# A trunk kernel on one core: vector and scalar work in instructions twice as wide

## The chip, the cores and the metric

The kernel runs on one core of a Trainium2 chip. A core has a matrix engine (TensorE, PE in the profile; its weight loads are listed apart as PEld), a vector engine (DVE), a scalar engine (ACT), GpSimd (POOL) and a queue engine (SP) that issues transfers. Each engine works through its own instructions in a fixed order and waits for the others at semaphores. The metric is the device time of one execution in microseconds (us), the median of several runs; lower is better.

## The reference

A decoder trunk of two layers over 256 tokens of width 1024, in float32. Cut to what matters:

```python
for l in range(DEPTH):                                      # 2 layers
    h = swiglu(x, w1[l, 0], w3[l, 0], w2[l, 0])             # (silu(x @ w1) * (x @ w3)) @ w2
    x = layernorm(ALPHA * x + 0.5 * h)
    h = mixer(x, l)
    x = layernorm(ALPHA * x + h)
    h = swiglu(x, w1[l, 1], w3[l, 1], w2[l, 1])
    x = layernorm(ALPHA * x + 0.5 * h)

def mixer(x):
    u, v, q, k, val, gates = split(x @ w_in)                # widths 1024, ..., 2 x 1024
    h_a = spatial_gate(gelu(u), layernorm(gelu(v)))         # 128x128 causal mixing of positions
    h_b = rmsnorm(diff_attention(rope(q), rope(k), val))    # 8 heads, two softmaxes subtracted
    g = sigmoid(gates + gate_b)
    return (g[0] * (h_a @ w_branch[0]) + g[1] * (h_b @ w_branch[1])) @ w_out
```

The hidden width of the SwiGLU is 2816. All weights are read once; nearly all arithmetic is in the matrix products.

## The kernel before

**Split products.** Each float32 operand is the sum of two rounded parts, hi and lo, and a product is hi·hi + lo·hi + hi·lo. The function `stream` fetches one transfer of weights, 128 partitions by up to 2048 float32 (1 MB), into a tile `raw` (four of them). It then splits it in two halves of 1024 columns: ACT copies a half into a tile `whi` (L166), DVE writes the rest, raw − whi, into a tile `wlo` (L168). There are eight tiles for hi halves and eight for lo halves, so a half's buffer is that of the same half four transfers earlier. With `sub=512` (in `gemm_b2`) each half is split in two pieces of 512.

**Projections by groups (`gemm_a2`).** x is held as `x_cat`, each k-tile with its 256 hi and 256 lo columns side by side. A group takes one or two transfers ("sources"), that is two or four halves, and each half has its own PSUM bank of 512 columns. First comes the hi phase: for each half eight matmuls of 512 columns (L220). Then the lo phase: for each half eight matmuls of 256 columns (L227) into the first half of the bank. After a half's last lo matmul ACT copies the bank's upper 256 columns to a tile r (L228) and DVE adds the lower 256 to it (L230, L232 where there is a scale). Four banks have the tag "main", so the bank of a half is free for the same half of the next group of two sources as soon as its add has run.

An FFN has 22 k-tiles of hidden width (FT). The first four come from `gemm_b2`, or from `gemm_first` at the start of the kernel, the other 18 from nine groups of two sources. After each source: silu on ACT (L523), the product on DVE (L524), and the split of the result into `hhi` (ACT, L173) and `hlo` (DVE, L174). Then two calls of `gemm_b`, one per half of the 1024 output columns, multiply by w2.

**`gemm_b`.** Both halves of the tokens (t = 0 and 1, 128 each) have a bank. The products of most k-tiles go to both in turn; the last k-tiles (tail, 4 unless the call says otherwise) are held back, and are done for t = 0 first, then `done(0)`, then for t = 1. In the FFN `done` reads the bank on DVE (L415, the residual and the first step of the norm). For the V projection of the mixer it is a Gelu on ACT (L688). `rows_b` issues the three products of a k-tile (L208).

**`gemm_b2`** does the same with four banks, two for each half of the tokens, and with the norm of the stage before running in its shadow. While that runs, some of its weight halves go to lent tiles of 512 columns from another pool (`lhi`, `llo`), since the normal ones aren't free yet. The norm's transposes (L474) are emptied by ACT into `xf` (L480), and `xf` is split into x (L173, L174).

**Mixer.** Eight rope groups of one source, then gates, V, u (groups of one source), the two branches (four groups of two sources), and the output by `gemm_b2`. Attention and the spatial gate run as side tasks: generators that issue a few instructions each time the main work has counted some beats (`beat`, `beside`). They use another four PSUM banks with the tag "side".

**Order.** PE's order is that of the program text. The order of DVE, ACT and POOL comes from a scheduler that goes by priorities (`step` raises them for each transfer), and `behind(...)` puts an instruction after a given one. SP issues the transfers.

Of the kernel before, what the change touches and what calls it, by code (L numbers as in the profile page):

```python
# [41 lines left out]
RAW, HL = 4, 8  # L42
# [8 lines left out]
def trunk(ctx, tc, x, xT, w13a, w13b, w2, wb, wqk, wa, wbr, wo, gateb, sgug, sgub, sguwT, sgubias, lam, diffg,  # L51
# [10 lines left out]
    act = ctx.enter_context(tc.tile_pool(name="act", bufs=27))  # L62
# [11 lines left out]
    def bank():  # L74
        return psum.tile([P, 512], F32, tag="main", name=name("bank"))
# [71 lines left out]
    def stream(src, width=CH, sub=HC, lent=(), after=(None, None)):  # L147
# [7 lines left out]
        for o in range(0, width, HC):  # L155
            if o // HC in lent:
                hi, lo = ([act.tile([P, 512], F32R, tag="slot", name=name(n)) for _ in range(2)] for n in ("lhi", "llo"))
                at = [(hi[j], lo[j]) for j in range(2)]
            else:
                hi = hi_pool.tile([P, HC], F32R, tag="hi", name=name("whi"))  # L160
                lo = lo_pool.tile([P, HC], F32R, tag="lo", name=name("wlo"))
                at = [(hi[:, p : p + sub], lo[:, p : p + sub]) for p in range(0, HC, sub)]
            for p, (h, w) in zip(range(0, HC, sub), at):
                r = raw[:, o + p : o + p + sub]
                with behind(latest[0]):
                    A.activation(h, r, AF.Copy)  # L166
                with behind(after[o // HC] or latest[1]):
                    V.tensor_tensor(out=w, in0=r, in1=h.bitcast(F32), op=ALU.subtract)  # L168
# [41 lines left out]
    def gemm_a2(srcs, xc, zs, rs=lambda: s512("r"), scale=1.0):  # L210
# [4 lines left out]
        for src in srcs:  # L215
            got += stream(src)
            for hi, _ in got[-2:]:
                b.append(bank())
                for k in range(KT):
                    PE.matmul(b[-1], hi[:, k * P : (k + 1) * P], xc(k), start=k == 0, stop=False)  # L220
                beat(0.65)
        for n, (_, lo) in enumerate(got):
            s = slice(n % 2 * T, (n % 2 + 1) * T)
            if n % 2 == 0:
                r, z = rs(), zs(n // 2)
            for k in range(KT):
                PE.matmul(b[n][:, :T], lo[:, k * P : (k + 1) * P], xc(k)[:, :T], start=False, stop=k == KT - 1)  # L227
            emptied[0] = A.activation(r[:, s], b[n][:, T:], AF.Copy, scale=scale).ins  # L228
            if scale == 1.0:
                a = V.tensor_tensor(out=z[:, s], in0=b[n][:, :T], in1=r[:, s], op=ALU.add)  # L230
            else:
                a = V.scalar_tensor_tensor(out=z[:, s], in0=b[n][:, :T], scalar=scale, in1=r[:, s], op0=ALU.mult,  # L232
                                           op1=ALU.add)
            added[0] = a.ins
            beat(0.35)
            if n % 2:
                yield n // 2, z
# [11 lines left out]
    def gemm_b(src, kts, xh, xl, done, tail=4, last=()):  # L249

        blocks = [[(bank(), c, n) for c, n in (last if t else ()) or ((0, 512),)] for t in range(NT)]
# [17 lines left out]
    def gemm_b2(srcs, xh, xl, done, norm=None):  # L269
# [3 lines left out]
        lent, after = [()] * 4, [(None, None)] * 4  # L273
        if norm:
            lent = [(0, 1), (0,), (), ()]
            after[1:3] = (None, norm.ends[0]), (norm.ends[0], norm.ends[0])
        ps = [[bank() for _ in range(2)] for _ in range(NT)]
# [16 lines left out]
    def gemm_first(srcs, done):  # L294

        step()
        ps = [[bank() for _ in range(2)] for _ in range(NT)]
        raw = [[raw_pool.tile([P, CH], F32, tag="raw", name=name("raw")) for _ in range(2)] for _ in range(2)]
        for k0, nk in ((0, 1), (1, 1), (2, 1), (3, 1), (4, 2), (6, 2)):
# [3 lines left out]
            if nk == 2 or k % 2 == 0:  # L303
                w = [[p.tile([P, HC], F32R, tag=n, name=name("w" + n)) for p, n in ((hi_pool, "hi"), (lo_pool, "lo"))]
                     for _ in range(2)]
# [187 lines left out]
    def ffn(l, f, i, norm, last=False):  # L493
# [26 lines left out]
        for j in range(FB, FT, 2):  # L520
            for m, z in gemm_a2([w13a[l, f, j - FB + m] for m in range(2)], both, lambda m: t512("silu")):
                s = z[:, :T]
                silu[0] = A.activation(s, s, AF.Silu).ins  # L523
                V.tensor_tensor(out=s, in0=s, in1=z[:, T:], op=ALU.mult)  # L524
                split(hh(j + m), hl(j + m), s)
                if norm is None and j + m == FB:
                    beside(setup(s[:, :1]), 0)
# [320 lines left out]
```

## Time and profile before

| | |
|---|---|
| median of 3 runs | 1243.45 us (1243.18 to 1244.18) |
| span of the profiled execution | 1242.5 us (its only time; 0.95 below the median) |
| PE busy | 1236.6 us, 6703 matmuls |
| DVE busy | 873.1 us, 1532 instructions |
| ACT busy | 756.0 us, 1388 instructions |
| POOL busy | 86.0 us |
| moved by DMA | 241.87 MB, 195 GB/s |

How to read it: busy time counts each engine by itself, and the engines run side by side. The span can't be shorter than the work of the engine that never rests. Matmuls overlap one another in a pipeline, so the step from one matmul's start to the next counts, not the duration of one record. In rows of the timeline the first number is the start, the second the time until the last of the xN instructions of that row ended, and in brackets stands the idle time of the engine before it and what ended it. In rows of groups the numbers after the first bar are the summed busy time and the mean nanoseconds of one.

### The profile page before, as it was taken

To read this page: it belongs to the slowest core of one execution; us is meant where nothing else is said; L and a number is where in the kernel's file an instruction comes from. 1 tells how busy PE (TensorE), PEld (TensorE's weight loads), DVE (VectorE), ACT (ScalarE), POOL (GpSimd) and SP (SyncE) were. 2 spreads that over 40 slices of the span, in tenths; PEclk is the share of its full clock that TensorE was granted. 3 is DMA by queue.
4 is the path that set the end of the run, shared out by engine and by line. 5 is a ranking of instruction groups with operands and counts; after the bars stand their busy time and mean duration, and the time that the engine had idled before them with its cause. 6 is when DMAs were issued, how large, how long until landed. Compare 5 with 4: busy or idle time off the path is not lost.

```text
span 1242.5 us, 17870 instructions
## 1 busy us (share of the span) xinstructions
PE 1236.6 (100%) x6703; PEld 1064.1 (86%) x6703; DVE 873.1 (70%) x1532; ACT 756.0 (61%) x1388; POOL 86.0 (7%) x184
## 2 busy tenths in 40 slices
PE   9999999999999999999999999999999999999998
PEld 8888888888888888888888888888888888888887
DVE  6766567876587977665677665679756879766753
ACT  6776446679665566664466664466786555766640
POOL 0100000144100000000000000002430000000000
PEclk9999999999999999999999999999999999999999
DMA  9765645654754745556545546556556456455540
GB/s 352 276 204 183 224 171 187 227 167 165 248 183 145 244 162 205 177 180 253 194 169 191 192 159 250 203 184 206 162 175 228 165 174 233 170 203 203 165 174 35
DMA packets 40679, 241.87 MB, mean 195 GB/s; under 512 B 5344, under 2 KB 6416, under 8 KB 14480
## 3 DMA queue, kind: packets, MB, share of 16 engines
q1 hardware_dynamic: 36624, 227.82, 52.1%
q0 software_dynamic: 3536, 12.13, 3.0%
q8 instruction: 52, 0.85, 0.3%
q10 hardware_dynamic: 432, 0.79, 0.2%
q14 instruction: 35, 0.29, 0.1%
HBM read 235.47 MB, written 1.05 MB: 190 GB/s over the span
## 4 chain that ended last, share of the span: by engine, by line
PE 99%; DVE 0%; ACT 0%; issue 0%; DVEq 0%; ACTq 0%
PE bank L220 38%; PE bank L208 35%; PE bank L227 20%; PE bank L323 2%; PE sbank L588 1%; PE sbank L474 1%; PE sbank L637 1%; PE sbank L718 1%; PE sbank L335 0%; PE sbank L635 0%; PE sbank L659 0%; PE sbank L508 0%; PE sbank L622 0%; PE sbank L627 0%; PE sbank L446 0%; DVE xtok L454 0%
## 5 line engine op out<-in xcount | busy, mean ns | idle before, releaser
L168 DVE TENSOR_TENSOR wlo<-raw,whi 128x1024 fp32r<-128x1024 f32 (+1 forms) x442 | 490.0, 1127 | 223.4 <-PE bank L227 129.3
L166 ACT ACTIVATE whi<-raw 128x1024 fp32r<-128x1024 f32 (+1 forms) x442 | 425.8, 978 | 279.4 <-PE bank L208 135.3
L220 PE MATMUL bank<-x,whi 128*128 128x512 f32 x1792 | 426.5, 392 | 0.0
L220 PEld LDWEIGHTS bank<-x,whi 128*128 128x128 f32 x1792 | 330.7, 188 | 69.0 <-issue 2.6
L227 PE MATMUL bank<-x,wlo 128*128 128x256 f32 x1792 | 229.9, 284 | 0.0
L227 PEld LDWEIGHTS bank<-x,wlo 128*128 128x128 f32 x1792 | 224.2, 191 | 4.8
L208 PE MATMUL bank<-whi,hhi 128*128 128x512 f32 (+1 forms) x374 | 141.3, 378 | 0.0
L208 PE MATMUL bank<-wlo,hhi 128*128 128x512 f32 (+1 forms) x374 | 141.0, 377 | 0.0
L208 PE MATMUL bank<-whi,hlo 128*128 128x512 f32 (+1 forms) x374 | 140.9, 377 | 0.0
L228 ACT ACTIVATE r<-bank 128x256 f32<-128x256 f32 x256 | 96.5, 380 | 66.0 <-PE bank L227 65.7
L208 PE MATMUL bank<-whi,x 128*128 128x512 f32 x328 | 106.6, 394 | 0.0
L208 PEld LDWEIGHTS bank<-whi,hlo 128*128 128x128 f32 x374 | 70.4, 188 | 13.0
L208 PEld LDWEIGHTS bank<-wlo,hhi 128*128 128x128 f32 x374 | 70.4, 188 | 12.7
L208 PEld LDWEIGHTS bank<-whi,hhi 128*128 128x128 f32 x374 | 70.4, 188 | 12.7
L208 PEld LDWEIGHTS bank<-whi,x 128*128 128x128 f32 x328 | 61.6, 188 | 12.7
L208 PE MATMUL bank<-wlo,x 128*128 128x512 f32 x164 | 64.0, 390 | 0.0
L480 ACT ACTIVATE xf<-sbank,ln_b,ln_g 128x128 f32<-128x128 f32 x80 | 30.0, 456 | 40.2 <-PE sbank L474 40.2
L230 DVE TENSOR_TENSOR silu<-bank,r 128x256 f32<-128x256 f32 x144 | 54.2, 418 | 0.2
L383 POOL DMA_DIRECT2D bc<-in_lng x6 | 3.2, 530 | 727.7 <-DVE bc L382 727.7
L415 DVE SCALAR_TENSOR_TENSOR xtok<-xtok,bank 128x512 f32<-128x512 f32 (+1 forms) x25 | 16.6, 663 | 42.2 <-PE bank L208 42.2
L564 POOL TENSOR_TENSOR swap<-swap,sin_t 128x512 f32<-128x512 f32 x16 | 24.3, 1517 | 242.4 <-DMA swap<-z 226.7
L208 PE MATMUL bank<-lhi,x 128*128 128x512 f32 x120 | 39.9, 396 | 0.0
(183 smaller groups left out, 1254.1 us busy)
## 6 DMA issues: line engine op xcount, KB each, us to landing
raw<-in_w13a SPq DMA_DIRECT2D x72, 1024.0 KB, 5.0
raw<-in_w SPq DMA_DIRECT2D x40, 1024.0 KB, 4.9
raw<-in_wa SPq DMA_DIRECT2D x24, 1024.0 KB, 5.5
raw<-in_wb SPq DMA_DIRECT2D x16, 1024.0 KB, 4.9
raw<-in_wqk SPq DMA_DIRECT2D x16, 1024.0 KB, 5.1
raw<-in_wbr SPq DMA_DIRECT2D x16, 1024.0 KB, 4.9
raw<-in_w13b SPq DMA_DIRECT2D x12, 1024.0 KB, 5.0
raw<-in_wo SPq DMA_DIRECT2D x8, 1024.0 KB, 4.9
```

Of the source, the lines that this page charges most:

```text
L166: A.activation(h, r, AF.Copy)
L168: V.tensor_tensor(out=w, in0=r, in1=h.bitcast(F32), op=ALU.subtract)
L208: PE.matmul(ps, xx, w, start=start and n == 0, stop=stop and n == 2)
L220: PE.matmul(b[-1], hi[:, k * P : (k + 1) * P], xc(k), start=k == 0, stop=False)
L227: PE.matmul(b[n][:, :T], lo[:, k * P : (k + 1) * P], xc(k)[:, :T], start=False, stop=k == KT - 1)
L228: emptied[0] = A.activation(r[:, s], b[n][:, T:], AF.Copy, scale=scale).ins
L230: a = V.tensor_tensor(out=z[:, s], in0=b[n][:, :T], in1=r[:, s], op=ALU.add)
L323: PE.matmul(ps[t][m], x[:, j, o + t * P : o + (t + 1) * P], y, start=k0 + j == 0 and o == 0 and y is hi, stop=k0 + j == KT - 1 and y is lo)
L415: V.scalar_tensor_tensor(out=self.y[t][:, s], in0=self.y[t][:, s], scalar=self.scale, in1=ps, op0=ALU.mult, op1=ALU.add)
L474: PE.transpose(b[:, k * P : (k + 1) * P], self.y[t][:, h * 512 + k * P : h * 512 + (k + 1) * P], ident)
L480: A.activation(xf[:, s], b[:, s], AF.Identity, scale=self.gT[:, f], bias=self.bT[:, f])
L564: turned_by[0] = G.tensor_tensor(out=s3, in0=s3, in1=s, op=ALU.mult).ins
```

## The change

- The tiles of `hi` and `lo` have 2048 columns, and there are four of each instead of eight. By default `stream` splits a whole transfer at once: one ACT copy and one DVE subtraction of 2048 columns. With `sub=512` pieces of 512 stay. The lent tiles are now given for whole transfers: the first two instead of one and a half. The pool they come from has 31 tiles instead of 27.
- `bank()` becomes `banks()`: one tile of two banks, two such tiles. In `gemm_a2` a source's two halves are the two banks of a tile, and r and the sum are made once for both (128x512 in two runs of 256).
- In the FFN, silu, product and split are done once for both sources of a group.
- In `gemm_b` the banks of t = 0 and t = 1 are the two banks of one tile (where the last call has two column blocks, a second tile is used).
- The matmuls, transfers and the order of PE's work are otherwise as before. `dynamic_dma_scratch_size=4096` is given to the program.

```diff
-RAW, HL = 4, 8
+RAW, HL = 4, 4
...
-    act = ctx.enter_context(tc.tile_pool(name="act", bufs=27))
+    act = ctx.enter_context(tc.tile_pool(name="act", bufs=31))
...
-    def bank():
-        return psum.tile([P, 512], F32, tag="main", name=name("bank"))
+    def banks():
+        return psum.tile([P, 2, 512], F32, tag="main", name=name("bank"), bufs=2)
...
-    def stream(src, width=CH, sub=HC, lent=(), after=(None, None)):
+    def stream(src, width=CH, sub=CH, lent=False, after=(None, None)):
...
-                hi = hi_pool.tile([P, HC], F32R, tag="hi", name=name("whi"))
-                lo = lo_pool.tile([P, HC], F32R, tag="lo", name=name("wlo"))
-                at = [(hi[:, p : p + sub], lo[:, p : p + sub]) for p in range(0, HC, sub)]
+                if o == 0:
+                    full = [p.tile([P, CH], F32R, tag=n, name=name("w" + n)) for p, n in ((hi_pool, "hi"), (lo_pool, "lo"))]
+                hi, lo = (v[:, o : o + HC] for v in full)
+                if sub == CH:
+                    at = [[v[:, :width] for v in full]][o:]
+                else:
+                    at = [(hi[:, p : p + sub], lo[:, p : p + sub]) for p in range(0, HC, sub)]
...
         for src in srcs:
             got += stream(src)
-            for hi, _ in got[-2:]:
-                b.append(bank())
+            b.append(banks())
+            for j, (hi, _) in enumerate(got[-2:]):
                 for k in range(KT):
-                    PE.matmul(b[-1], hi[:, k * P : (k + 1) * P], xc(k), start=k == 0, stop=False)
+                    PE.matmul(b[-1][:, j], hi[:, k * P : (k + 1) * P], xc(k), start=k == 0, stop=False)
                 beat(0.65)
-        for n, (_, lo) in enumerate(got):
...
+        for n, ps in enumerate(b):
+            r, z = rs(), zs(n)
+            for j, (_, lo) in enumerate(got[2 * n : 2 * n + 2]):
+                for k in range(KT):
+                    PE.matmul(ps[:, j, :T], lo[:, k * P : (k + 1) * P], xc(k)[:, :T], start=False, stop=k == KT - 1)
+                if j == 0:
+                    beat(0.35)
+            r2, z2 = (v.rearrange("p (j t) -> p j t", j=2) for v in (r, z))
+            emptied[0] = A.activation(r2, ps[:, :, T:], AF.Copy, scale=scale).ins
             if scale == 1.0:
-                a = V.tensor_tensor(out=z[:, s], in0=b[n][:, :T], in1=r[:, s], op=ALU.add)
+                a = V.tensor_tensor(out=z2, in0=ps[:, :, :T], in1=r2, op=ALU.add)
...
-        blocks = [[(bank(), c, n) for c, n in (last if t else ()) or ((0, 512),)] for t in range(NT)]
+        b = banks()
+        blocks = [[(b[:, 0], 0, 512)]]
+        if last:
+            b2 = banks()
+            blocks.append([((b, b2)[c > 0][:, 1], c, n) for c, n in last])
+        else:
+            blocks.append([(b[:, 1], 0, 512)])
...
         if norm:
-            lent = [(0, 1), (0,), (), ()]
+            lent = [True, True, False, False]
...
+            z = tmp.tile([P, 2, 2, T], F32, tag="pair", name=name("z"), bufs=1)
+            for _ in gemm_a2([w13a[l, f, j - FB + m] for m in range(2)], both, lambda m: z[:, m].rearrange("p j t -> p (j t)")):
+                pass
+            s = z[:, :, 0]
+            silu[0] = A.activation(s, s, AF.Silu).ins
+            V.tensor_tensor(out=s, in0=s, in1=z[:, :, 1], op=ALU.mult)
+            split(*(v[j // 2].rearrange("p (k t) -> p k t", k=2) for v in (h_hi, h_lo)), s)
```

What this does to DVE's order in a steady FFN group. Names carry a running number; `wlo` is the lo part of a transfer that is used two groups later, `bank` the PSUM tile, `r` ACT's copy of its upper columns, and in brackets stands whose semaphores the instruction waits for. DVE before:

```order
L168 TENSOR_TENSOR wlo_1175<-raw_1172,whi_1174 128x1024 [waits DMAHW0_49,PE_49]
L230 TENSOR_TENSOR silu_1013<-bank_966,r_1012 128x256 [waits Activation_49]
L230 TENSOR_TENSOR silu_1013<-bank_975,r_1012 128x256 [waits Activation_49]
L168 TENSOR_TENSOR wlo_1179<-raw_1172,whi_1178 128x1024
L524 TENSOR_TENSOR silu_1013<-silu_1013 128x256 [waits DVE_49,Activation_49]
L230 TENSOR_TENSOR silu_1039<-bank_994,r_1038 128x256 [waits Activation_49]
L230 TENSOR_TENSOR silu_1039<-bank_1003,r_1038 128x256 [waits Activation_49]
```

The same place on DVE after the change:

```order
L172 TENSOR_TENSOR wlo_1122<-raw_1119,whi_1121 128x2048 [waits DMAHW2_49,PE_49,Activation_49]
L236 TENSOR_TENSOR z_940<-bank_947,r_987 128x512 [waits DVE_49,Activation_49]
L236 TENSOR_TENSOR z_940<-bank_970,r_1006 128x512 [waits Activation_49]
L172 TENSOR_TENSOR wlo_1145<-raw_1142,whi_1144 128x2048 [waits DMAHW3_49]
L536 TENSOR_TENSOR z_940<-z_940 128x2x256 [waits Activation_49]
```

Before, a split of 1024 columns stands ahead of the first add, and it waits for PE; now a split of 2048 columns stands there, and the add behind it empties two banks.

PE at the end of the tail of an FFN's `gemm_b`, where the token half changes from t = 0 to t = 1. Before (bank 1592 is that of t = 0, 1593 that of t = 1):

```order
L208 MATMUL bank_1592<-whi_1694,hhi_155 128x512
L208 MATMUL bank_1592<-wlo_1695,hhi_155 128x512
L208 MATMUL bank_1592<-whi_1694,hlo_166 128x512
L208 MATMUL bank_1593<-whi_1664,hhi_149 128x512
L208 MATMUL bank_1593<-wlo_1665,hhi_149 128x512
L208 MATMUL bank_1593<-whi_1664,hlo_160 128x512
```

After (one tile, 1390, for both):

```order
L212 MATMUL bank_1390<-whi_1471,hhi_155 128x512
L212 MATMUL bank_1390<-wlo_1472,hhi_155 128x512
L212 MATMUL bank_1390<-whi_1471,hlo_166 128x512
L212 MATMUL bank_1390<-whi_1453,hhi_149 128x512 [waits DVE_49]
L212 MATMUL bank_1390<-wlo_1454,hhi_149 128x512
L212 MATMUL bank_1390<-whi_1453,hlo_160 128x512
```

The first matmul of t = 1 now waits for DVE; the instruction that it waits for is the read of the tile's other bank.

38 lines of the change are left out of this document (13 added, 25 removed).

## The prediction

> **What bounds the kernel now.** I read the busy line, the chain, the timeline of one FFN group, and then the groups that stand beside it. The first:
>
> ```profile
> span 1242.5 us, 17870 instructions
> PE 1236.6 (100%) x6703; PEld 1064.1 (86%) x6703; DVE 873.1 (70%) x1532; ACT 756.0 (61%) x1388; POOL 86.0 (7%) x184
> PE 99%; DVE 0%; ACT 0%; issue 0%; DVEq 0%; ACTq 0%
> ```
>
> PE is the bound: busy 1236.6 of 1242.5 us, and the chain is PE. All time in which PE does nothing is 5.9 us, so that is the most that smoother vector work can return as long as the matmuls keep their pace. DVE is at 70% and ACT at 61%; shortening them gives nothing by itself. The question is what the regrouped work does to PE's waits.
>
> One steady FFN group, PE alone and then all engines:
>
> ```profile
> 477.21 4.00 PE L227 MATMUL bank<-x,wlo 128*128 128x256 f32 x32
> 481.04 7.44 PE L220 MATMUL bank<-x,whi 128*128 128x512 f32 x32
> 488.32 4.00 PE L227 MATMUL bank<-x,wlo 128*128 128x256 f32 x32
> ...
> 488.52 1.06 ACT L166 ACTIVATE whi<-raw 128x1024 fp32r<-128x1024 f32 x1 [0.75 <-PE bank L220]
> 489.47 1.23 DVE L168 TENSOR_TENSOR wlo<-raw,whi 128x1024 fp32r<-128x1024 f32 x1 [3.81 <-PE bank L227]
> 490.62 0.75 DVE L230 TENSOR_TENSOR silu<-bank,r 128x256 f32<-128x256 f32 x2
> 491.28 1.22 DVE L168 TENSOR_TENSOR wlo<-raw,whi 128x1024 fp32r<-128x1024 f32 x1
> 492.15 1.32 PE L220 MATMUL bank<-x,whi 128*128 128x512 f32 x5
> ```
>
> A group is 32 wide matmuls with the hi weights, 7.28 us (481.04 to 488.32: 0.227 each), then 32 narrow ones with the lo weights, 3.83 us (488.32 to 492.15: 0.120 each), 11.11 together, and PE goes on without a gap. DVE, which had nothing to do, starts the next wlo 1.15 us into the lo phase: the eighth narrow matmul, which reads that buffer last, started at 488.32 + 7 × 0.120 = 489.16, so the release takes 0.31. Two adds take 0.75 us from 490.62 on; the first, which frees the first bank, ends at about 491.0, 1.1 us before PE needs the bank at 492.15. That 1.1 us is the slack of the present order.
>
> The durations:
>
> ```profile
> L168 DVE TENSOR_TENSOR wlo<-raw,whi 128x1024 fp32r<-128x1024 f32 x360 | 436.7, 1227 | 213.1 <-PE bank L227 126.8 <-ACT whi L166 70.7 <-issue 15.2
> L168 DVE TENSOR_TENSOR wlo<-raw,whi 128x512 fp32r<-128x512 f32 x82 | 53.3, 687 | 10.3 <-issue 7.9 <-PE bank L227 2.4
> L166 ACT ACTIVATE whi<-raw 128x1024 fp32r<-128x1024 f32 x360 | 378.2, 1059 | 225.8 <-PE bank L220 125.8 <-PE bank L208 91.5 <-ACT hhi L173 3.1
> L166 ACT ACTIVATE whi<-raw 128x512 fp32r<-128x512 f32 x82 | 47.5, 625 | 53.6 <-PE bank L208 43.8 <-PE bank L220 9.5
> L415 DVE SCALAR_TENSOR_TENSOR xtok<-xtok,bank 128x512 f32<-128x512 f32 x23 | 15.7, 684 | 39.1 <-PE bank L208 39.1
> L688 ACT ACTIVATE vg<-bank 128x512 f32<-128x512 f32 x8 | 4.8, 599 | 5.1 <-PE bank L208 5.1
> L688 ACT ACT_TABLE_LOAD x2 | 2.6, 1283 | 0.0
> ...
> 482.97 2.36 DVE L168 TENSOR_TENSOR wlo<-raw,whi 128x1024 fp32r<-128x1024 f32 x2
> ```
>
> **The wide split.** From 512 to 1024 columns the DVE subtract grows by 540 ns, so 2048 take about 1227 + 1080 = 2307 ns; four times 540 (2.16, no fixed part) and twice 1227 (2.45) bound it. Two in a row take 2.36, so the second starts 1.13 after the first, 0.09 before its end: the next instruction follows the wide one after about 2.22. In the same way ACT's 2048 is 1059 + 868 = 1.93 us (1.74 to 2.12). An add of 128x512 with a PSUM operand has its nearest row in L415: 0.68. By these rows the change saves on DVE 2 × 1.23 − 2.31 = 0.15 us a transfer, on ACT 0.19. That is worth nothing: PE covers it, and it waits for neither engine now.
>
> The Trainium skill ("Perfetto Trace Analysis", "Optimizing Scalar/DVE Operations") says that grouping into larger operations helps if the engine is saturated, and that where ScalarE and VectorE are not saturated but cause bubbles elsewhere, breaking instructions up lets work finish sooner. The DVE share of 70% puts this kernel in the second case, so by that rule too the sign is a loss.
>
> **FFN groups (the main term).** After the change DVE's order at the end of a group is: wlo of 2048 columns, add of the first tile, add of the second, wlo, multiply, hlo. Let L be the start of the lo phase.
> - The wlo writes the lo buffer that all 16 narrow matmuls of the first source read, not eight: it starts at L + 15 × 0.120 + 0.31 = L + 2.11 (now L + 1.15). The queue's order is fixed, so nothing passes it.
> - The add of the first tile stands behind it: L + 2.11 + 2.22 = L + 4.33, end at L + 5.01. ACT's copy r for it is ready: the whi ahead of it starts at L + 0.20 as at 488.52, ends at L + 2.13, and r (0.60) at L + 2.73.
> - The next group's first matmul writes that two-bank tile. There are two such tiles, so it waits for the add. PE resumes 0.13 after a DVE end (the boundary rows below: DVE ends 188.56 + 0.69 = 189.25, matmul at 189.38): L + 5.14, where it needs L + 3.84.
>
> So PE stalls 1.30 us a group. The second tile's add ends 0.6 later, while PE fills the first tile for 3.6 us: hidden. The period becomes 12.4 us, in which DVE has about 2 × 2.22 + 4 × 0.6 = 6.8 us: it catches up each time, and the stall neither grows nor heals. With 2.16 or 2.45 for the wide subtract it is 1.15 or 1.45. An FFN has 9 groups, four FFNs 36. In four of them, the first of each FFN, a piece hlo of 128x256 also stands ahead of the add:
>
> ```profile
> 38.12 0.42 DVE L174 TENSOR_TENSOR hlo<-sbank,hhi 128x256 fp32r<-128x256 f32 x1
> 38.46 0.75 DVE L230 TENSOR_TENSOR silu<-bank,r 128x256 f32<-128x256 f32 x2
> ...
> 178.91 0.39 PE L208 MATMUL bank<-whi,hhi 128*128 128x512 f32 x1
> 179.11 0.69 DVE L415 SCALAR_TENSOR_TENSOR xtok<-xtok,bank 128x512 f32<-128x512 f32 x1 [8.98 <-PE bank L208]
> ...
> 186.35 1.50 ACT L480 ACTIVATE xf<-sbank,ln_b,ln_g 128x128 f32<-128x128 f32 x4 [0.65 <-PE sbank L474]
> 188.56 0.69 DVE L174 TENSOR_TENSOR x<-xf,x 128x512 fp32r<-128x512 f32 x1 [1.08 <-ACT x L173]
> 188.93 0.39 PE L208 MATMUL bank<-lhi,x 128*128 128x512 f32 x1
> 189.38 0.65 PE L208 MATMUL bank<-lhi,x 128*128 128x512 f32 x2
> ```
>
> It takes 0.34 until the next starts (38.12 to 38.46), so these stall 1.64. Sum: 32 × 1.30 + 4 × 1.64 = 48.2 us (42 to 54 by the bounds). The mixer's four branch groups per layer have the same tiles; there one stands like an FFN group (1.30), one has 0.44 more work of PE behind it (0.86), and two have only two 512-wide pieces in front of the add, 2 × 0.60: 2.11 + 1.20 + 0.68 + 0.13 − 3.84 = 0.28 each. That is 2.7 a layer, 5.5 for two (0 if the neighbours cover it, 10.4 if all eight stall 1.30). The groups of one source wait for an add of the group before the last, with the whole next group (5.55 us) between: nothing.
>
> **The tails of the down projections.** The banks of the two token halves are now one tile, and the order shows the first matmul of the second half's tail waiting for DVE, which reads the first half's bank in that tile. Now PE runs straight on: at 178.91 it starts the second half, at 179.11 L415 reads the first. Then it must wait: 0.20 + 0.69 + 0.13 = 1.02 us, twice per FFN, eight times: 8.2 us. It is not hidden, since PE's queue has nothing else ahead. Bounds: 0, were the wait already met, and 8 × (1.02 + 2.22) if each L415 had a wide wlo in front of it. I take the place that the order gives, with none in front. The V projection waits in the same way for ACT's Gelu: 0.20 + 0.60 + 0.13 = 0.93 for the second half of columns; for the first the table load of 1.28 comes in between, up to 2.21, part of which (I take 0.5) passes while a whi copy and matmuls end: some 2.35 per layer, 4.7 in all (3.7 to 6.3).
>
> **The norm boundaries.** Where an FFN's norm feeds the next projection, x arrives just in time: DVE's x ends at 189.25, and the matmul at 189.38 follows. After the change four 512-wide whi pieces, which wait for a buffer of 2048 columns, stand in ACT's queue ahead of xf; I put x about 0.45 later, an estimate between nothing and one piece (0.63). Three places: 1.4 us (0 to 1.9).
>
> **The mixer's side work.** Attention steps (scores, softmax, transposes) pass through the same DVE and ACT queues. A step that finds itself behind a wide piece starts up to 2.31 − 1.23 = 1.08 us later. Eight head pairs in both layers with three hand-overs give at most 26 us, at least nothing, and a little below nothing if the saved 0.15 us arrives there. Tasks are spread over a group or more, so I lie near the low end: 2. DMAs are as many and as large as before, on the same queues; the smaller scratch for POOL's descriptors touches only loads that it issues long before use. Both: 0.
>
> **Sum.** 48.2 + 5.5 + 8.2 + 4.7 + 1.4 + 2 = 70.0 us on the profiled span of 1242.5, so 1312.5. The median of the runs, 1243.45, lies 0.95 above that span: 1313.4.
>
> **The rivals.**
>
> *Not slower: the matmuls get quicker.* The sum holds if a matmul costs what it costs now. Were the spacing limited by the vector engines' traffic, fewer and wider instructions could shorten it. 70 us over 6703 matmuls is 10.4 ns each; from there on the kernel is no slower (1243). Against it speaks a stretch in which both vector engines are idle:
>
> ```profile
> core 0: us, PE busy (x) PEld busy (x) DVE busy (x) ACT busy (x) POOL busy (x), PEclk, DMA share, GB/s
> 171.00:179.00 8.00, 8.00 (x37) 6.64 (x36) 0.00 (x0) 0.00 (x0) 0.00 (x0) 1.00 0.65 273
> ...
> 4.92 2.01 PE L323 MATMUL bank<-whi,x 128*128 128x512 f32 x4
> 6.77 0.63 PE L323 MATMUL bank<-wlo,x 128*128 128x512 f32 x2
> ```
>
> A record lasts 0.39, so a window of 8.00 us touches (8.00 + 0.39) / 0.227 = 37.0 of them: exactly the 37 counted. With DVE and ACT silent the spacing is the same 0.227 as in the group above, where both work. Chance 0.05. The Trainium skill ("TensorE: Matmul & The Clock Gate", "Wait — 56ns, not 53.3ns?") gives 215.7 ns for a warm matmul of 512 columns; by that figure 11 ns per wide matmul would be there to win, and the trace disagrees with it: 227 ns, vector engines idle or not.
>
> *Much slower: the clock falls at each wait.* At the start PE's four wide matmuls take 1.85 us (4.92 to 6.77), 0.46 each instead of 0.23, so a relapse of that length costs 0.9. On some 52 waits that is 47 us more, 1360. Against it: a wait of 1.3 in 12.4 us leaves PE busy for 90%; but the granted clock of 1.00 comes from stretches without such waits, so the trace doesn't exclude it. Chance 0.04.
>
> *The mixer pays more.* 10 to 26 us instead of 2, by the bound above: 1321 to 1337, in the middle 1329. For it: attention already waits on chains of small steps. Chance 0.15.
>
> *Only the groups pay.* The tails, branches and boundaries are covered after all, and the wide subtract is as short as 2.16: 1243.5 + 42 to 50, so 1286 to 1294. Against it: the waits stand in the order. Chance 0.10.
>
> **How the numbers follow.** My own sum holds with 0.66; its range, from the bounds of the subtract (±6), the V tail, the boundaries and the first few us of the mixer, is 1302 to 1324, and its middle is the prediction, 1313. To reach 0.8 I add the nearer parts of two rivals: down to 1292, up to 1336. Within 0.2%, 2.5 us, a measurement could not tell it from no change: 0.02. Faster 0.03, both from the first rival; slower 0.95.
>
> **What would show it.** In the profile after: PE's busy time nearly the same, its idle time 60 to 80 us; in the list of PE's waits DVE's add with some 40 times 1.3 us and L415's successor with eight times 1.0; wlo of 2048 columns at 2.3 us; a group period of 12.4 us; DVE's and ACT's busy time lower by some 40 and 60 us. Wrong would be: no wait of PE for the adds (DVE doing them ahead of the wlo), a wide matmul at less than 0.22 us, a granted clock under 1, or the largest wait in the mixer.

## The result, and the profile after

The changed kernel takes 1345.34 us (median of four runs, 1344.98 to 1346.59), the kernel before 1243.36: a ratio of 1.082, 95% interval 1.0805 to 1.0836. The direction was right; 1313 was 32 us too low, and the range ended at 1336.

The head of the profile's page and its chain, after:

```profile
span 1344.9 us, 16970 instructions
PE 1260.1 (94%) x6703; PEld 1068.0 (79%) x6703; DVE 851.3 (63%) x1156; ACT 702.4 (52%) x1012; POOL 86.8 (6%) x184
PE 75%; issue 8%; DVE 7%; ACT 5%; DMA 2%; POOL 2%; SPq 1%; DVEq 0%; ACTq 0%; POOLq 0%
```

DVE has become 21.8 us less busy and ACT 53.6, with a quarter fewer instructions. PE now rests 84.8 us instead of 5.9, and its own busy time has grown by 23.5 with the same 6703 matmuls. The list of PE's waits after (in total, how often, the longest):

```profile
PE bank L224 <- DVE z L236: 38.1, 32, 1.7
PE sbank L601 <- ACT aT L637: 14.2, 2, 7.1
PE bank L212 <- DVE xtok L425: 6.2, 8, 0.8
PE bank L212 <- DVE z L236: 4.5, 4, 1.1
PE bank L212 <- ACT vg L701: 3.8, 4, 1.2
PE sbank L601 <- DVE qk L581: 3.5, 4, 1.6
PE sbank L672 <- ACT on L667: 3.4, 4, 1.6
PE bank L224 <- DVE bz L236: 2.6, 4, 1.1
```

Five of the eight rows are waits that the prediction named. The list counts PE's idle time alone, which lies below the forecast terms (38.1 and 4.5 us for the groups, against 48.2); the table below has what each stage lost. The second row was not foreseen: two waits of 7.1 us, one in each mixer. The sixth and the seventh (3.5 and 3.4 us) belong to the mixers' side work too, for which 2 us were put down in all.

The waits don't add up to the loss, so I laid the two traces side by side: PE's order is the same (all 6703 matmuls and transposes agree in line and shape), hence the n-th of one is the n-th of the other, and the difference of their starts can be followed through the kernel. Its growth by stage, in us, for all parts of a kind together:

| stage | predicted | after |
|---|---|---|
| 36 FFN groups | 48.2 | 52.4 |
| FFN down projections (tails) | 8.2 | 8.7 |
| V projection | 4.7 | 5.0 |
| branches | 5.5 | 5.2 |
| norm boundaries | 1.4 | 0.7 |
| mixer's output and its norm | 0 | 1.6 |
| mixer from the norm to the V projection (attention) | 2 | 29.0 |
| start | 0 | -0.2 |
| sum | 70.0 | 102.4 |

The group, in the timeline after (start, time until the last of the xN ends; in brackets the idle time before it and what ended it):

```profile
528.29 3.99 PE L230 MATMUL bank<-x,wlo 128*128 128x256 f32 x32
528.49 1.92 ACT L170 ACTIVATE whi<-raw 128x2048 fp32r<-128x2048 f32 x1 [1.71 <-PE bank L224]
530.46 2.29 DVE L172 TENSOR_TENSOR wlo<-raw,whi 128x2048 fp32r<-128x2048 f32 x1 [4.75 <-ACT whi L170]
532.67 1.28 DVE L236 TENSOR_TENSOR z<-bank,r 128x512 f32<-128x512 f32 x2
533.41 1.89 PE L224 MATMUL bank<-x,whi 128*128 128x512 f32 x7 [1.13 <-DVE z L236]
```

With L = 528.29 the wide split starts at L + 2.17 (forecast 2.11), the add at L + 4.38 (4.33), PE at L + 5.12 (5.14). The wide subtract takes 2.29 us where 2.307 was estimated. The row names ACT's copy `whi` as what released the split last, where the prediction had PE's sixteenth matmul; the two come so close together that the time is the same: the copy ends at L + 2.12, and in e6, with ACT's copies in halves, the split starts at L + 2.17 again and the row names PE. After the wait the second matmul starts late too, by some 0.11 us (the restart, below), so a group loses 1.40. At the end of a tail:

```profile
168.73 0.69 DVE L425 SCALAR_TENSOR_TENSOR xtok<-xtok,bank 128x512 f32<-128x512 f32 x1 [1.15 <-PE bank L212]
169.47 0.50 PE L212 MATMUL bank<-whi,hhi 128*128 128x512 f32 x1 [0.78 <-DVE xtok L425]
```

PE stands still until DVE has read the other bank of the tile. And the wait that was not seen coming, in the first mixer:

```profile
296.50 0.60 PE L635 MATMUL sbank<-ident,pp 128*128 128x128 f32 x4
...
299.88 0.67 PE L601 MATMUL sbank<-qk,qk 64*128 64x256 f32 x2 [0.66 <-DVE qk L581]
...
300.49 2.30 DVE L172 TENSOR_TENSOR wlo<-raw,whi 128x2048 fp32r<-128x2048 f32 x1
...
300.74 2.14 POOL L204 TENSOR_SCALAR nwa<-nwa 128x4 f32<-128x4 f32 x1
...
305.25 0.20 POOL L205 TENSOR_TENSOR nwy<-nwa,nwy 128x4 f32<-128x4 f32 x1
305.48 1.28 ACT L667 ACTIVATE on<-on,nwy 128x128 f32<-128x128 f32 x4 [3.16 <-POOL nwy L205]
...
307.02 0.58 ACT L637 ACTIVATE aT<-sbank 128x512 f32<-128x512 f32 x1
...
307.65 2.07 PE L601 MATMUL sbank<-qk,qk 64*128 64x256 f32 x6 [7.10 <-ACT aT L637]
```

PE's transposes end at 297.1, and the copy aT that empties their bank could follow. It runs ten us later, because in ACT's fixed queue it stands behind `on`, the normalisation of the head pair before, which waits for a chain of small steps on POOL (the reciprocal root) that ends at 305.45. In the kernel before, the same copy stands ahead of that `on`:

```profile
280.21 0.58 ACT L624 ACTIVATE aT<-sbank 128x512 f32<-128x512 f32 x1
...
289.44 1.27 ACT L654 ACTIVATE on<-on,nwy 128x128 f32<-128x128 f32 x4
```

Windows of two FFN groups, of this wait and of what follows it (busy time of each engine, then the granted clock):

```profile
core 0: us, PE busy (x) PEld busy (x) DVE busy (x) ACT busy (x) POOL busy (x), PEclk, DMA share, GB/s
507.00:532.00 25.00, 22.43 (x127) 19.73 (x128) 13.91 (x14) 12.22 (x12) 0.00 (x0) 1.00 0.49 168
...
301.00:307.00 6.00, 0.00 (x0) 0.00 (x0) 2.79 (x3) 2.84 (x9) 3.71 (x10) 0.76 0.86 318
307.50:313.50 6.00, 5.85 (x16) 3.79 (x16) 1.69 (x9) 3.24 (x12) 0.00 (x0) 0.50 0.00 0
```

In the FFN groups the clock stays at 1.00 through their waits. After the long wait it is at half for six us: another 3.1 us in the first mixer, 2.8 in the second.

### The profile page after: what moved, and what is told of

The parts are those of the page before. It is cut to its first block, busy times and chain, and to the rows that moved or that the text cites. A ratio compares the mean times of both kernels' runs of the same rounds, so it can differ in the third digit from the quotient of the medians.

```text
span 1344.9 us, 16970 instructions
## 1 busy us (share of the span) xinstructions
PE 1260.1 (94%) x6703; PEld 1068.0 (79%) x6703; DVE 851.3 (63%) x1156; ACT 702.4 (52%) x1012; POOL 86.8 (6%) x184
## 3 DMA queue, kind: packets, MB, share of 16 engines
HBM read 235.47 MB, written 1.05 MB: 176 GB/s over the span
## 4 chain that ended last, share of the span: by engine, by line
PE 75%; issue 8%; DVE 7%; ACT 5%; DMA 2%; POOL 2%; SPq 1%; DVEq 0%; ACTq 0%; POOLq 0%
PE bank L224 32%; PE bank L212 32%; PE bank L230 8%; ACT whi L170 3%; DVE wlo L172 2%; DVE z L236 2%; DMA swap<-z 1%; DMA raw<-in_w13b 1%; PE sbank L601 1%; PE sbank L484 1%; DMA raw<-in_w13a 1%; POOL nwa L204 1%; DVE qk L581 1%; SPq L573 1%; POOL swap L577 0%
## 5 line engine op out<-in xcount | busy, mean ns | idle before, releaser
L172 DVE TENSOR_TENSOR wlo<-raw,whi 128x2048 fp32r<-128x2048 f32 (+2 forms) x256 | 460.2, 1808 | 308.3 <-ACT whi L170 274.7
L170 ACT ACTIVATE whi<-raw 128x2048 fp32r<-128x2048 f32 (+2 forms) x256 | 384.8, 1524 | 271.8 <-PE bank L212 144.7
L224 PE MATMUL bank<-x,whi 128*128 128x512 f32 x1792 | 433.5, 396 | 38.2 <-DVE z L236 38.1
L234 ACT ACTIVATE r<-bank 128x512 f32<-128x512 f32 x128 | 76.1, 595 | 67.7 <-PE bank L230 57.9
L212 PE MATMUL bank<-whi,x 128*128 128x512 f32 x288 | 94.9, 396 | 3.8 <-ACT vg L701 3.8
L212 PEld LDWEIGHTS bank<-wlo,hhi 128*128 128x128 f32 x374 | 70.4, 188 | 12.5
L212 PEld LDWEIGHTS bank<-whi,x 128*128 128x128 f32 x288 | 54.1, 188 | 16.4 <-ACT vg L701 5.5
L177 ACT ACTIVATE hhi<-z 128x512 fp32r<-128x512 f32 x36 | 22.7, 632 | 74.1 <-DVE z L536 74.1
L212 PE MATMUL bank<-wlo,x 128*128 128x512 f32 x144 | 56.2, 390 | 0.0
L212 PE MATMUL bank<-lhi,x 128*128 128x512 f32 x160 | 52.4, 396 | 0.0
L236 DVE TENSOR_TENSOR z<-bank,r 128x512 f32<-128x512 f32 x80 | 51.6, 683 | 0.0
L611 ACT ACTIVATE pp<-pp,mx 128x256 f32<-128x256 f32 (+1 forms) x64 | 28.3, 444 | 31.9 <-DVE mx L609 31.9
```

What stands on the lines that cost most here:

```text
L177: a = A.activation(hi, src, AF.Copy)
L212: PE.matmul(ps, xx, w, start=start and n == 0, stop=stop and n == 2)
L224: PE.matmul(b[-1][:, j], hi[:, k * P : (k + 1) * P], xc(k), start=k == 0, stop=False)
L234: emptied[0] = A.activation(r2, ps[:, :, T:], AF.Copy, scale=scale).ins
L236: a = V.tensor_tensor(out=z2, in0=ps[:, :, :T], in1=r2, op=ALU.add)
L611: A.activation(p[:, s], p[:, s], AF.Exp, bias=mx[:, a], scale=-1.0, accum_out=sums[:, a])
```

## The experiments

Theory A, from the prediction and the trace: the loss is made of separate waits, each from one place in a fixed queue or one shared tile. The wide split ahead of the add makes the group waits; the tile of two banks makes the tail waits; the place of aT in ACT's queue makes the mixer's. Rival B: the two-bank tiles and their joint adds are late by themselves; or the side work is slow as a whole, and a wait that is taken away turns up elsewhere. A change of one thing at a time tells them apart.

With each measured time stand, in brackets, its ratio to the kernel before and the 95% interval of the ratio. The growth of the delay against the kernel before by stage, for the changed kernel and all runs but e8, worked out as above from the profiled executions (which lie up to 2.7 us from the medians):

| | groups | tails | V | branches | attention | all |
|---|---|---|---|---|---|---|
| after | 52.4 | 8.7 | 5.0 | 5.2 | 29.0 | 102.4 |
| e1 adds first | 0.0 | 8.6 | 5.0 | 1.4 | 17.5 | 35.4 |
| e2 tiles apart | 52.8 | 0.1 | 0.0 | 5.3 | 33.1 | 94.6 |
| e3 aT ahead of on | 52.7 | 8.7 | 5.0 | 5.3 | 19.6 | 93.3 |
| e4 halves | 13.0 | 8.7 | 5.2 | 2.2 | 8.8 | 39.7 |
| e5 one-bank tiles | 34.4 | 0.1 | 0.0 | 2.7 | 4.4 | 43.0 |
| e6 wide on DVE only | 51.0 | 8.6 | 5.1 | 5.2 | 6.5 | 78.7 |
| e7 wide on ACT only | 14.1 | 8.6 | 5.0 | 2.1 | 10.0 | 42.0 |
| e9 aT first | 52.8 | 8.7 | 5.0 | 5.2 | 15.5 | 89.3 |
| e10 three repairs, wide DVE | 0.0 | 4.8 | 0.0 | 1.4 | 23.2 | 31.5 |
| e11 three repairs, halves | 0.0 | 7.5 | 0.0 | 0.0 | 21.6 | 31.7 |

The start, the norms, the gates and the mixer's output, together 1.4 to 3.3 us, are left out. "Attention" ends a little after PE's first matmuls of the V projection, which matters for e2, e10 and e11.

**e1: the adds ahead of the wide split.**

```diff
-        out = []
+        out, first = [], None
+        if not lent:
+            first = owners[-HL].get("add")
+            owners.append({})
...
-                with behind(after[o // HC] or latest[1]):
+                with behind(after[o // HC] or latest[1]), behind(first):
...
-            added[0] = a.ins
+            added[0] = own[n]["add"] = a.ins
```

`first` is the add that empties the bank of the source whose buffer is taken over.

> The changed kernel, with one thing moved: on DVE the split of a transfer stands behind the add that empties the bank of the source whose buffer it takes over. All instructions keep their widths. Theory A (the wide split in front of the add costs the group its 1.40 us): the first add can then run at L + 2.73 (when r is ready), ends at L + 3.41, and PE needs it at L + 3.84, so the 36 FFN waits (52.0 us) and most of the branch waits (5.2) go: 1345.3 - 52 - 4 = about 1289. Rival B (the add of two banks comes too late by itself, wherever the split stands): the waits stay above 0.8 us each, the time above 1318.

Measured: 1279.7 us (1.0292, 1.0276 to 1.0307). The timeline of its group:

```profile
514.29 4.00 PE L235 MATMUL bank<-x,wlo 128*128 128x256 f32 x32
514.49 1.92 ACT L174 ACTIVATE whi<-raw 128x2048 fp32r<-128x2048 f32 x1 [1.19 <-PE bank L229]
516.40 0.60 ACT L239 ACTIVATE r<-bank 128x512 f32<-128x512 f32 x1
517.03 0.69 DVE L241 TENSOR_TENSOR z<-bank,r 128x512 f32<-128x512 f32 x1 [3.01 <-ACT r L239]
517.64 2.28 DVE L176 TENSOR_TENSOR wlo<-raw,whi 128x2048 fp32r<-128x2048 f32 x1
518.12 4.04 PE L229 MATMUL bank<-x,whi 128*128 128x512 f32 x17
```

The add runs at L + 2.74, as soon as r is there, and PE starts the next group at L + 3.83 without a wait. Not one instruction is narrower: the two-bank tile with its single add and the wide split each cost a group nothing; their order does. That settles 52 us for theory A. The remaining 9 us below the expectation are in attention (17.5 instead of 29.0): with other anchors the scheduler lays out the side work another way too. In this run all copies aT stand ahead of `on`, as in the kernel before, and yet attention loses 17.5 us; the longest wait there is now 3.0 us in each mixer, for `pp` on DVE.

**e2: gemm_b with a tile for each token half.**

```diff
-        b = banks()
+        b, b2 = banks(), banks()
...
-            blocks.append([(b[:, 1], 0, 512)])
+            blocks.append([(b2[:, 0], 0, 512)])
```

> The changed kernel, with the two token halves of gemm_b in two tiles instead of the two banks of one. Theory A: the eight waits at the FFN tails (1.07 each, 8.6 us) and the four of the V projection (4.9 us) go, the rest stays: 1345.3 - 13.5 = 1332. Rival: PE would wait there anyway, for a buffer or a split that is late behind the widened work; then 1340 to 1345.

Measured: 1340.2 us (1.0786, 1.0764 to 1.0807). The FFN tails' 8.7 us are gone, so the shared tile makes them. The V projection's two waits for Gelu are gone as well, but a new one has come:

```profile
PE bank L212 <- DVE gz L236: 5.6, 2, 2.8
```

gemm_b now takes both tiles at its start, and the second is still being emptied from the last gate group. With two tiles in all, a wait is moved rather than removed there. The expectation missed by 8, and the time lies at the lower end of the rival's range: for the V projection the rival was right, for the tails it was not.

**e3: aT ahead of `on`, by an anchor.**

```diff
-            A.activation(aT0, b[:, :T], AF.Copy)
+            copied[0] = A.activation(aT0, b[:, :T], AF.Copy).ins
...
-                with behind(emptied[0]):
+                with behind(emptied[0]), behind(copied[0]):
```

> The changed kernel, with ACT's normalisation of the attention output (on, which waits for POOL's reciprocal root) put behind the copies aT of the next head pair. Theory A (the 7.1 us wait of PE in each mixer is an inversion in ACT's queue: aT stands behind on): both waits go (7.27 + 6.95), and with them the stretch at half clock after each (3.1 + 2.8): 1345.3 - 20 = 1325, mean clock 1.00. Rival B (attention is slow because every step passes behind wide pieces, and PE would wait somewhere else): 1338 to 1345.

Measured: 1338.3 us (1.0764, 1.0746 to 1.0782): a miss, and inside rival B's range. By the medians 7.0 of the expected 20 us came; in the table attention loses 19.6 instead of 29.0. The timeline shows why:

```profile
299.01 2.31 DVE L172 TENSOR_TENSOR wlo<-raw,whi 128x2048 fp32r<-128x2048 f32 x1
...
301.24 0.47 DVE L678 SCALAR_TENSOR_TENSOR hb<-sbank,dgs,hb 128x256 fp32r<-128x256 f32 x1
...
301.75 0.47 ACT L677 ACTIVATE hb<-sbank,dgs 128x256 fp32r<-128x256 f32 x1 [0.91 <-DVE hb L678]
...
302.12 0.59 ACT L637 ACTIVATE aT<-sbank 128x512 f32<-128x512 f32 x1
```

aT no longer waits for POOL, but it stands behind the second half of `hb` on ACT. That waits for DVE's first half of `hb`, which stands behind a wide split from 299.01 to 301.3. PE's wait shrank from 7.1 to 3.7 us, and the clock fell after it all the same. So the inversion was one reason, and the wide piece in a queue another.

**e9: aT ahead of `on`, `hb` and r.** The second answer to e3: as there, and `hb` is issued after a pause of 0.7 beats and behind aT.

```diff
+            yield 0.7
...
-                A.activation(h[:, :T], b[:, s], AF.Copy, scale=dl)
+                with behind(copied[0]):
+                    A.activation(h[:, :T], b[:, s], AF.Copy, scale=dl)
```

> The changed kernel, with ACT's copies aT of a head pair put ahead of three things of the pair before: its normalisation on, which waits for POOL, its result hb, whose second half waits for DVE behind a wide split, and the copy r. Theory A (what costs 20 us in the two mixers is the place of aT in ACT's queue; putting it ahead of on alone, as the run before did, left it behind hb): PE's long wait goes, and with it the stretch at half clock: 9 us of attention loss instead of 29, 1325, mean clock 1.00. Rival B (the side work as a whole runs late behind wide pieces, so PE waits for the next step instead): the loss stays above 18 us, 1335 and more.

Measured: 1334.1 us (1.0728, 1.0712 to 1.0744): nearer to rival B's 1335 than to 1325. The wait for aT is 1.5 us now, but PE waits 2.1 for `on` ahead of it, and attention still loses 15.5 us, between the 9 of theory A and the 18 of rival B. So this edit takes away 13.5 of the 29.0 (11.2 us by the medians), with the clock's part in them. Of what is left, PE's list of waits has 10.2 us: 3.7 for `on`, 2.9 for aT, 2.5 for `qk` and 1.1 for `hb`; each mixer also has a stretch at half clock. Why each of these steps is late is not shown.

**e4: splits of 1024 columns, in tiles of 2048.**

```diff
-    def stream(src, width=CH, sub=CH, lent=False, after=(None, None)):
+    def stream(src, width=CH, sub=HC, lent=False, after=(None, None)):
```

> The changed kernel, with each transfer split again in two pieces of 1024 columns (in the same tiles of 2048); two-bank tiles, joined adds and joined gating stay. Theory A: the piece ahead of the first add waits for eight matmuls only and takes 1.14, so the add isn't late: the group and most branch waits go (56 us), and if ACT's queue isn't inverted there either, the 20 us of the mixer; the tails and the V projection stay. 1345.3 - 56 - 20 = 1269, or 1289 with the inversion. Rival B (the two-bank tile and its one add are what costs): above 1320.

Measured: 1284.9 us (1.0332, 1.0317 to 1.0348), 16 above the expectation. Of the group:

```profile
491.40 3.99 PE L230 MATMUL bank<-x,wlo 128*128 128x256 f32 x32
...
493.57 1.23 DVE L172 TENSOR_TENSOR wlo<-raw,whi 128x1024 fp32r<-128x1024 f32 x1 [4.43 <-issue]
...
494.71 0.68 DVE L236 TENSOR_TENSOR z<-bank,r 128x512 f32<-128x512 f32 x1
...
495.45 0.73 PE L224 MATMUL bank<-x,whi 128*128 128x512 f32 x2
```

I had the narrow piece start after eight matmuls, at L + 1.15. It starts at L + 2.17: the tile is still 2048 columns wide, and its release waits for all sixteen. The row itself doesn't name the releaser; the sixteenth matmul starts at L + 15 × 0.120 = L + 1.80, and with the 0.31 of the release that gives L + 2.11 (in e5 below, where the row names PE, the split starts at L + 2.12). The size of the tile sets when the split may start, the size of the instruction only how long it holds the queue. What is left of the wait is 0.34 in most groups, restart included, 13.0 in all. The copies aT stand ahead of `on` here.

**e5: tiles of one bank, with the wide split kept.**

```diff
-        return psum.tile([P, 2, 512], F32, tag="main", name=name("bank"), bufs=2)
+        return [psum.tile([P, 512], F32, tag="main", name=name("bank")) for _ in range(2)]
...
+                emptied[0] = A.activation(r[:, s], ps[j][:, T:], AF.Copy, scale=scale).ins
+                    a = V.tensor_tensor(out=z[:, s], in0=ps[j][:, :T], in1=r[:, s], op=ALU.add)
```

> The changed kernel with the two-bank tiles taken back: four tiles of one bank, copies and adds of 256 columns per half, gemm_b with a bank for each token half; splits of 2048 columns, four wide tiles and the joined gating stay. Theory A (the wide split is what costs): the split still stands ahead of the adds, so the group waits to L + 2.11 + 2.22 + 0.42 + 0.13 = L + 4.88 where it needs L + 3.84: 1.04, with 0.11 at the restart 1.15, 36 times 41 us; branches 4; the mixer's attention 10 to 29; tails and V projection nothing: 1298 to 1318. Rival B (two-bank tiles are what costs): below 1275.

Measured: 1287.6 us (1.0354, 1.0338 to 1.0369), 10 below the expected span, since attention loses only 4.4, and above the rival's 1275. The groups:

```profile
490.23 3.99 PE L230 MATMUL bank<-x,wlo 128*128 128x256 f32 x32
...
492.35 2.29 DVE L172 TENSOR_TENSOR wlo<-raw,whi 128x2048 fp32r<-128x2048 f32 x1 [2.33 <-PE bank L230]
...
494.55 1.41 DVE L234 TENSOR_TENSOR z<-bank,r 128x256 f32<-128x256 f32 x4
495.03 7.55 PE L224 MATMUL bank<-x,whi 128*128 128x512 f32 x32 [0.80 <-DVE z L234]
```

The wait is still there: PE starts at L + 4.80 instead of L + 3.84, 0.96 late, and with the restart such a group loses 1.07. The wide split makes it with one-bank tiles too. That is 0.33 less than in the changed kernel (1.40), since the first add empties one bank; and at the first group boundary of each FFN there is no wait here.

**e6 and e7: wide on one engine only.** The transfer's other half of the split runs in two instructions of 1024.

```diff
# e6: ACT in two pieces                         # e7: DVE in two pieces
-                    A.activation(h, r, AF.Copy)
+                    for q in cuts:
+                        A.activation(h[:, q], r[:, q], AF.Copy)
...
-                    V.tensor_tensor(out=w, in0=r, in1=h.bitcast(F32), op=ALU.subtract)
+                    for q in cuts:
+                        V.tensor_tensor(out=w[:, q], in0=r[:, q], in1=h[:, q].bitcast(F32), op=ALU.subtract)
```

> The changed kernel with ACT's copies of a transfer in two instructions of 1024 columns; DVE's subtraction stays at 2048. Theory A: the group waits hang on DVE's width alone, so 1.40 x 36 and the tails stay, as does what attention loses to DVE's wide pieces: 1330 to 1345. If ACT's width made the loss in attention, its 20 us go: 1322 to 1328. Rival (ACT's width delays the copy r and so the add): the group waits shrink below 1.0, the time under 1315.

> The changed kernel with DVE's subtraction of a transfer in two instructions of 1024 columns; ACT's copy stays at 2048. Theory A: the group waits fall to the 0.34 that the run with halves on both engines showed (12 us instead of 52), tails and V projection stay (13.5): 1285 if attention loses to DVE's pieces alone (9 us as there), 1305 if ACT's do it. Rival (ACT's width): 1320 and more.

Measured: 1321.9 us (1.0627, 1.061 to 1.0645) and 1285.7 (1.0337, 1.0322 to 1.0353). The group waits are DVE's: 51.0 with DVE wide, 14.1 with ACT wide. e6 lies 8 us below what theory A gave it, e7 where expected. In attention neither width costs much alone (6.5 and 10.0, against 29.0 with both): ACT's queue holds aT ahead of `on` in both. So the 29.0 cannot be divided between the engines. Nor do two wide engines alone make it: e5 has both, with one-bank tiles, aT stands ahead of `on`, and attention loses 4.4; e1 has both and the two-bank tiles, with other anchors, aT stands ahead, and it loses 17.5. Among these runs the swap is there only in the changed kernel and in e2, which have wide splits on both engines, two-bank tiles and the original anchors.

**e8: the joint gating alone**, on the kernel before (silu, product and split once for both sources).

> The kernel before, with one part of the change alone: silu, product and split once for both sources of an FFN group (and the smaller scratch, which makes room for it). By every theory here it is off the path, since DVE and ACT have the whole next group for it: 1243.4, within 2 us.

Measured: 1243.68 us; ratio 1.000 (0.9991 to 1.001). This part of the change is free.

**e10 and e11: the repairs together**, e1's order and e2's tiles with ACT in halves (e10) or both engines in halves (e11).

> Three repairs together on the changed kernel: the wide split on DVE behind the add whose buffer it takes over, tiles apart in gemm_b, and ACT's copies of a transfer in two pieces of 1024 (DVE's subtraction stays at 2048). Theory A: groups 0, FFN tails 0, V 0 to 5, branches 1.4, mixer 6 as with ACT's halves alone, output and norms 3: 1243.8 + 10 to 16 = 1254 to 1260. Below 1243 by no theory, since PE's idle time before was 5.9 us in all. If the losses of the mixer don't add that way: up to 1275.

> The same with splits of 1024 columns on both engines (in tiles of 2048); two-bank adds, joint gating, adds ahead of the split, tiles apart in gemm_b. Theory A: groups 0, tails 0, V 0 to 5, branches 1, mixer 9 as with halves alone, the rest 3: 1243.8 + 13 to 18 = 1257 to 1262. If the mixer's loss came from the late release of the wide tiles, the same; if from the two-bank adds alone, also the same, so this run only shows whether the repairs add up.

Measured: 1275.7 us (1.0258, 1.0243 to 1.0274) and 1273.1 (1.0224, 1.0202 to 1.0246), both above the expectation, e10 at its outer case of 1275. The groups are at 0.0, but the waits of two-tile gemm_b come back at other starts: 4.8 and 7.5 us at the FFN down projections, and at the V projection PE waits up to 4.2 us for the last gate group's gz, with the clock at half after it (in the table under attention). That is what rival B said of waits that turn up elsewhere. No version here beats the kernel before; the part e8 equals it.

## Why the prediction was right in part and wrong in sum

- **PE is the bound, and saved vector time is worth nothing**: right. DVE and ACT lost 75 us of work together (DVE 21.8, where some 40 had been forecast), and the kernel became slower; e8, which saves only such work, 13.6 us of it, moved the time by nothing.
- **FFN groups**: right in the mechanism, shown by e1 (order alone removes it) and e5 (it outlives the two-bank tile). The size was 48.2 and came to 52.4. Nearly all of the 4.2 us missing are a cost that I had not counted: after a wait the second matmul starts 0.11 late too, so a group loses 1.40 where the wait is 1.28.
- **Tails, V projection, branches**: right within half a us each, in part by luck. The waits of the tails were 0.94 where 1.02 was forecast, and the uncounted restart made up for it. The branch group put at 0.86 waited 0.34, and four restarts a layer filled most of the gap. The V term doesn't follow from its own working: 0.5 taken off 2.21 leaves 1.71, so 2.64 a layer and 5.3 in all, not 4.7; the runs gave 1.36 and 0.85 a layer, each with a restart of 0.11.
- **Norm boundaries**: 0.7 instead of 1.4; in its place the mixer's output norm lost 1.6, which I gave no term.
- **The mixer's side work is the step that failed.** I took 2, with 26 as the upper bound, by pricing each hand-over at one wide piece more (1.08 us). It was 29.0. I followed the order of the queues at the group and at the tail, and counted only widths in the mixer. There the copies aT had changed places with `on` in ACT's queue, which put a whole chain through POOL, not one piece, before PE's next step. Those two waits (14.2) and the half clock after them (5.9) are some 20 of the 29.0; most of the rest is shorter waits for `qk` and `on`, 3.5 and 3.4. With the 4.2 of the groups, these 27 us more than forecast are nearly all that the sum is short of. The prediction's own signs of being wrong, the largest wait in the mixer and a granted clock under 1, both came. The swap is not all of it: in e1, without it, attention still lost 17.5. That the rival "the mixer pays more" had this end right, 10 to 26, doesn't save the range: its bound rested on the same pricing.
- **The rival of the clock** was put at 0.9 us per wait on all 52 waits. The short waits cost no clock (1.00 in the window above). After the long ones it costs about 3 us each, 5.9 in the two mixers, and none of the sum had that.
- **The rival of quicker matmuls** is out: where PE doesn't wait, the spacing is as before (in e1's group, without a wait, the 32 narrow matmuls take 3.83 us again, 0.120 each).

Not settled: why the scheduler puts `on` ahead of aT just in the changed kernel and e2, and why attention still loses between 4.4 us (e5) and 23.2 us (e10, with the waits at the V projection) where it doesn't.

## What to carry to other kernels

Where one engine is the bound, look at an instruction of another engine not by its length but by what stands behind it in its queue and who waits for that: the same wide split cost 52 us ahead of an add and nothing behind it. A bigger tile is released later and couples its parts, whatever the instructions on it. And when widths change, compare the order of every engine's queue in every stage, side work above all: a single swap there came with a wait of 7.1 us and a stretch at half clock in each mixer, where I had put 2 us for both.

## What the runs showed of the hardware that was not expected

**A wait of PE can halve the clock for some us afterwards, and its length alone doesn't say whether.** Waits of 1.3 us every 12.5 left it at 1.00. Around 2 us it went either way: after 2.1 in e9 the matmuls kept their pace, after 1.9 in e2 and 2.0 in e4 they did not. In e9 the clock fell after a wait of 1.5 us, and in e2 it stayed after one of 2.8. First two windows of the changed kernel, after the 1.6 us wait that ends at 293.6 and around the end of the 7.1 us wait:

```profile
293.60:297.00 3.40, 3.14 (x17) 2.47 (x18) 0.16 (x1) 3.40 (x9) 0.77 (x1) 1.00 0.02 5
304.10:314.30 10.20, 6.65 (x22) 4.58 (x22) 2.04 (x9) 5.26 (x17) 1.01 (x5) 0.50 0.23 94
```

Then after the wait of 2.0 us in e4, the one of 1.5 in e9 and the one of 2.8 in e2:

```profile
281.50:285.50 4.00, 3.94 (x13) 3.23 (x14) 3.96 (x9) 3.94 (x12) 0.00 (x0) 0.57 0.01 4
...
301.90:305.30 3.40, 3.40 (x9) 2.48 (x8) 0.76 (x2) 0.99 (x5) 1.75 (x9) 0.50 0.85 277
...
351.30:355.30 4.00, 3.95 (x17) 3.30 (x18) 0.00 (x0) 0.91 (x2) 0.00 (x0) 1.00 0.71 260
```

In the clock records of these traces every stretch at half inside the kernel lasts 3.41 us, or two or three times that (10.24 after each of the long waits of the changed kernel), and the stretches at full speed between them are whole multiples too (655.36 us, 192 times 3.413, in the changed kernel). So the clock changes on a grid of its own. What decides in each case is not settled.

The Trainium skill ("TensorE: Matmul & The Clock Gate", "What's actually happening") lets the clock fall after an idle window of about 3.4 us that runs freely. The falls here after waits of 1.5 to 2.0 us come earlier than it says; that 2.1 us and more could also pass without one, and the steps of 3.41 us, would suit a window that runs freely.

**A small POOL step stands still beside a wide DVE instruction.** POOL's L204 takes 0.22 us by itself, and 2.14 from 300.74 on, beside the split of 300.49 to 302.79 (rows above); it ends 0.1 after it. In the kernel before, a POOL step beside a split of half the width took 1.28:

```profile
279.79 1.28 POOL L198 TENSOR_TENSOR nwa<-nwy 128x4 f32<-128x4 f32 x1
279.79 1.22 DVE L168 TENSOR_TENSOR wlo<-raw,whi 128x1024 fp32r<-128x1024 f32 x1
```

So the width of DVE's instruction sets how long one step of POOL is held up. The chain as a whole loses about the same, since beside the narrower pieces it was held twice (1.28 and 1.05 us): its steps from `ve` to the last `nwy` took 5.9 us before (278.06 to 283.93) and 6.2 after (299.28 to 305.45). The Trainium skill ("Perfetto Trace Analysis", "Optimizing Scalar/DVE Operations") says that GpSimd and DVE share a read port which a DVE operation can hold alone; the rows agree.
